# Attention logits on 64 rows of TensorE for each head, in a two-layer decoder trunk on one core

## The chip, the cores and the metric

The kernel runs on one core of a Trainium2 chip. A core has TensorE (PE, the matrix engine; PEld are its weight loads), VectorE (DVE), ScalarE (ACT), GpSimd (POOL) and the queue that issues transfers (SP). The metric is the device time of one launch in microseconds (us); lower is better. Where a number of several runs is given, it is the median.

## The reference

The program is a trunk of two layers on one sequence of 1024 tokens with 1024 channels. Layer 0 is dilated sliding-window attention, layer 1 a state-space layer, each with a gate and with a norm before and behind it. The change is in the logits of layer 0 alone. There are 16 heads of 64 channels and three groups of windows; each group has its own queries, keys and values.

```
DILATED_GROUPS = ((128, 1), (512, 4), (2048, 16))
...
proj = h @ w_in
for g, (window, dilation) in enumerate(DILATED_GROUPS):
    # query t attends to t - j*dilation, j = 0..window/dilation
    logits = einsum('bnqrhe,bnkrhe->bnrhqk', q, k) * HEAD_DIM ** -0.5 + bias
    lse = logsumexp(logits);  p = exp(logits - lse);  o = p @ v
wts = softmax(stack(lses))            # over the three groups
o = sum(wts * outs);  return (o * silu(z)) @ w_out
```

## The kernel before

All matrix products are computed in parts: an operand x is split into a rounded part hi and a rest lo, and a product is hi·hi + hi·lo + lo·hi, three passes of PE (`split`, L79, makes the parts: ACT copies hi, DVE subtracts to get lo).

After a first stage that makes all values (about the first 350 us), `attn_pair` (L652) runs for p = 0 to 7, a pair of heads each, and in it three window groups g. A group projects the queries and then the keys of its two heads: two halves of 512 tokens each, and for a half 24 matmuls of 512 columns in `proj_part` (L110), into a bank of the two-bank pool `psj`. A bank comes free again when `evac_q` (L190) or `evac_k` (L204) has copied it out. The 128 partitions of such a bank are the 64 channels of the first head and the 64 of the second.

`evac_q` and `evac_k` lay the parts out so that one matmul over 128 rows does two of the products. For g = 0 and 1, the tile `qh` holds in its rows the hi part of head 0 above the lo part of head 0, and `ql` the lo part of head 1 above the hi part of head 1; `kh[:, s]` holds the hi keys of head s twice, one copy in each half of the rows, and `kl[:, s]` the lo keys of head s in its own half and zeros in the other. For g = 2 both heads' queries lie one above the other, and the keys of a head have zeros in the other head's rows (`zero_other`, L217, on POOL). `c.kh` and `c.kl` are one buffer each, used by every group in turn.

`attn_unit` (L463) makes the logits of four query tiles of 128 tokens (j = 0 to 3), twice for each group. A tile sees 256 keys, or 128 at a window's edge. For g = 0 and 1 it takes four matmuls (L485), two for each head; for g = 2 three, over both heads at once. They write one bank of the two-bank pool `psl`. DVE then adds the bias and takes the maximum (L488), ACT does the exponential (L499), PE transposes the weights (L510), ACT and DVE split them (`split_weights`), and PE multiplies them with the values (L559, L585).

The order on each engine is made by a scheduler from the program's dependencies and its own estimates; what stands in `with c.tc.high_priority(AHEAD)` is taken earlier than its place in the program. Every engine then works through its own list in order. In the list, projections of a later group fill PE between the logits, transposes and value products of an earlier one. Behind the last pair stands the gate (L800, L801), whose projections also use `psj`.

Of the kernel before, what the change touches and what calls it, by code (L numbers as in the profile page):

```python
# [15 lines left out]
F32 = mybir.dt.float32  # L16
# [24 lines left out]
def f32(ap):  # L41
    return ap.bitcast(F32)
# [146 lines left out]

def evac_q(c, ps, g, t0, q):  # L190


    nc = c.nc
    n = ps.shape[1] // ORD[g]
    at = (S - t0) // ORD[g] - n
    sv = ps.rearrange("p (l r) -> p r l", r=ORD[g])[:, :, ::-1]
    q = [t.rearrange("p (r l) -> p r l", r=ORD[g])[:, :, at:at + n] for t in q]
    a, b = HEADS
# [5 lines left out]
def evac_k(c, ps, g, t0, kh, kl):  # L204


    n = ps.shape[1] // ORD[g]
    at = t0 // ORD[g]
    sv = ps.rearrange("p (l r) -> p r l", r=ORD[g])
# [7 lines left out]
def zero_other(c, t):  # L217

    for s in range(2):
        rows = HEADS[1 - s]  # L220
        c.nc.gpsimd.tensor_copy(t[rows, s, :], c.zt[rows].to_broadcast([64, S]))


def load_first(c, a, k):
# [233 lines left out]
def ms_col(g, n, h, qt):  # L458

    return (n * 16 + h * 8 + 7 - qt, n * 16 + h * 8 + (qt ^ 1), n * 16 + h * 8 + qt)[g]  # L460


def attn_unit(c, g, u, q, k, v, bt, ms, O):  # L463


    nc = c.nc
    qh, ql = q
    kh, kl = k
    lg = c.attn.tile([P, 2, 4, 256], F32, tag="lg", name="lg", bufs=3)
    tiles = []  # L470
    for j in range(4):
        qt = u * 4 + j
        m = (7 - qt, 1 - qt % 2, 0)[g]
        start = (max(m - 1, 0) * P, qt // 2 * 256, qt * P)[g]
        w = 256 if m else 128
        tiles.append(w)
        ps = c.psl.tile([P, 2, 256], F32, tag="psl", name="psl")
        qs = slice(qt * P, qt * P + P)
        ks = slice(start, start + w)
# [6 lines left out]
        for h in range(2):  # L486
            col = ms_col(g, 0, h, qt)
            nc.vector.tensor_tensor_reduce(  # L488
                lg[:, h, j, 0:w], ps[:, h, 0:w], bt[:, h, 256 - w:256], scale=1.0, scalar=-3.0e38,
                op0=ALU.add, op1=ALU.max, accum_out=ms[:, col:col + 1])  # L490
    nm = c.small.tile([P, 2, 4], F32, tag="nm", name="nm")
    at = (4 - 4 * u, 4 * u, 4 * u)[g]
    mx = ms[:, 0:16].rearrange("p (h t) -> p h t", h=2)[:, :, at:at + 4]
    nc.vector.tensor_scalar(nm, mx, -1.0, None, op0=ALU.mult)  # L494
    for h in range(2):
        for j, w in enumerate(tiles):
            col = ms_col(g, 1, h, u * 4 + j)
            b = (3 - j, j ^ 1, j)[g]
            nc.scalar.activation(lg[:, h, j, 0:w], lg[:, h, j, 0:w], AF.Exp, bias=nm[:, h, b:b + 1],  # L499
                                 accum_out=ms[:, col:col + 1])  # L500
    (pv_last if g == 2 else pv_first)(c, g, u, lg, v, O)
    if u == 1:
        put_ms(c, g, ms)
# [148 lines left out]
def attn_pair(c, p, w_in, h):  # L652
    nc = c.nc
    c.pair = p
    O = []
    for g in range(3):
        qh = c.attn.tile([P, S], F32R, tag="qh", name="qh", bufs=2)
        ql = c.attn.tile([P, S], F32R, tag="ql", name="ql", bufs=2)
        w = load_w(c, w_in[g * 8 + p])
        for th in range(2):  # L660
            src = proj_half(c, w, h[th])
            with c.tc.high_priority(AHEAD):
                evac_q(c, src, g, th * H, (qh, ql))
        bt = load_bias(c, p, g)
        if g == 2:
            zero_other(c, c.kh)
        w = load_w(c, w_in[(3 + g) * 8 + p])
        for th in range(2):
            src = proj_half(c, w, h[th])
            with c.tc.high_priority(AHEAD):  # L670
                evac_k(c, src, g, th * H, c.kh, c.kl)
        v = load_v(c, p, g)
        rotations(c, p, g)
        if g == 1:
            run_merge(c)
        ms = c.small.tile([P, 32], F32, tag="ms", name="ms")
        for u in range(2):
            attn_unit(c, g, u, (qh, ql), (c.kh, c.kl), v, bt, ms, O)
# [31 lines left out]
def attention(c, a):  # L710
# [8 lines left out]
    with tc.tile_pool(name="vphase", bufs=1, side="right", reuse_waits="tile") as pool:  # L719
# [21 lines left out]

        v_phase(c, a, rows)

    c.attn = c.es_attn.enter_context(tc.tile_pool(name="attn", bufs=1, side="right", reuse_waits="tile"))
    c.kh = c.attn.tile([P, 2, S], F32R, tag="kh", name="kh")
    c.kl = c.attn.tile([P, 2, S], F32R, tag="kl", name="kl")
    zt = c.cst.tile([P, 1], F32, name="zt")
    nc.vector.memset(zt, 0.0)
    c.zt = zt
    zero_other(c, c.kl)  # L750
    c.w_engine = nc.gpsimd
    for p in range(8):
        attn_pair(c, p, a["w_in"], h)
# [702 lines left out]
def trunk(tc, a):  # L1456
# [4 lines left out]
    with ExitStack() as es:  # L1461
# [8 lines left out]
        c.psl = pool("psl", bufs=2, space=PSUM)  # L1470
        c.pst = pool("pst", bufs=2, space=PSUM)
        c.pso = pool("pso", bufs=2, space=PSUM)
        c.dr = pool("dr", bufs=1, space=DRAM)
        dram = lambda name, shape: c.dr.tile(shape, F32, name=name)
        c.vec_dr = dram("vec_dr", [3, 16, 384])
# [24 lines left out]
        c.es_attn = es.enter_context(ExitStack())  # L1500
        h = attention(c, a)
        c.es_attn.close()
        c.pb = es.enter_context(tc.tile_pool(name="pb", bufs=1, side="right", reuse_waits="tile"))
        g, raw = attn_gate(c, a, h)
        z112 = c.outs.tile([P, D], F32, tag="O", name="z112", bufs=4)[:, 0:8 * 112]
# [111 lines left out]
```

## Time and profile before

| | |
|---|---|
| median of 3 runs | 1727.71 us (1724.31 to 1729.69) |
| profiled execution: time, span | 1722.86 us, 1721.1 us |
| PE busy | 1655.9 us, 96% of the span |
| DVE, ACT, POOL busy | 1064.8, 799.9, 483.5 us |
| attention stage | about 350 to 1156 us |

The span is the time from the first to the last instruction of the profiled execution. In the rows further down a line names the source line, the engine, the operation, the tile written and the tiles read, and after that the shape. For matmuls a pair like 128*128 stands before the shape: the rows and columns of PE that the instruction uses. A matmul's duration contains its way through the array, so that durations of neighbours overlap; the distance from one start to the next tells what it occupies.

### The profile page before, as it was taken

The page shows a single profiled execution, that of the slowest core. Times are in us where ns is not written, and L with a number is a line of the kernel's source. Part 1 is how long each engine was busy: PE and PEld are TensorE (multiplying, and loading weights), DVE is VectorE, ACT ScalarE, POOL GpSimd, SP SyncE. Part 2 cuts the span into 40 slices and gives each one's busy share as a digit, 9 for nine tenths or more (in the row PEclk, how much of TensorE's full clock was granted, in tenths as well). Part 3 has the DMA queues.
Part 4 walks back from the last instruction along what each step waited for, and adds up shares of the span by engine and source line. Part 5 has one row for each costly group of instructions (what it writes and reads, how often), then busy time and mean ns, then how long its engine had stood idle before and what let it go on. Part 6 is the DMA issues. An engine that isn't in the chain of part 4 may idle for free. (4 is left out here: it accounts for less than half of the span.)

```text
span 1721.1 us, 25792 instructions
## 1 busy us (share of the span) xinstructions
PE 1655.9 (96%) x9262; PEld 1415.1 (82%) x9262; DVE 1064.8 (62%) x2582; ACT 799.9 (46%) x1872; POOL 483.5 (28%) x321
## 2 busy tenths in 40 slices
PE   6999999999999999999999999988998999989998
PEld 5889999988888788888888888876886887867886
DVE  7698798735566556566555565557462777764533
ACT  5232222246656656656756756653442232243411
POOL 2000000041242432524342442405210344413121
PEclk9999999999999999999999999999999999999999
DMA  6223454441242323323232423327259766465432
GB/s 236 91 52 102 137 181 154 128 144 53 55 111 80 87 80 91 88 74 105 79 107 73 116 81 98 112 71 200 86 166 232 206 211 219 139 186 167 141 122 86
DMA packets 176900, 212.68 MB, mean 124 GB/s; under 512 B 37361, under 2 KB 133380, under 8 KB 176772
## 3 DMA queue, kind: packets, MB, share of 16 engines
q1 hardware_dynamic: 176772, 211.04, 40.9%
q8 instruction: 73, 1.20, 0.3%
q14 instruction: 55, 0.45, 0.1%
HBM read 154.03 MB, written 56.96 MB: 123 GB/s over the span
## 5 line engine op out<-in xcount | busy, mean ns | idle before, releaser
L110 PE MATMUL psj<-hh,whi 128*128 128x512 f32 x896 | 360.4, 402 | 16.2 <-ACT kh L214 8.5
L110 PE MATMUL psj<-hh,wlo 128*128 128x512 f32 x896 | 359.6, 402 | 0.3 <-POOL wlo L84 0.3
L110 PE MATMUL psj<-hl,whi 128*128 128x512 f32 x896 | 357.9, 399 | 0.0
L110 PEld LDWEIGHTS psj<-hh,whi 128*128 128x128 f32 x896 | 169.8, 189 | 51.6 <-ACT kh L214 10.6
L84 POOL TENSOR_TENSOR wlo<-wraw,whi 128x1024 fp32r<-128x1024 f32 x48 | 115.4, 2405 | 335.7 <-ACT whi L83 329.4
L110 PEld LDWEIGHTS psj<-hh,wlo 128*128 128x128 f32 x896 | 169.6, 189 | 35.8 <-POOL wlo L84 0.7
L110 PEld LDWEIGHTS psj<-hl,whi 128*128 128x128 f32 x896 | 169.8, 190 | 33.5
L499 ACT ACTIVATE lg<-lg,nm 128x128 f32<-128x128 f32 (+1 forms) x384 | 168.1, 440 | 18.9 <-DVE nm L494 18.0
L83 ACT CAST whi<-wraw 128x1024 fp32r<-128x1024 f32 x80 | 83.8, 1047 | 141.9 <-PE psj L110 97.4
L488 DVE CUSTOM_DVE_ANT_0 lg<-psl,T 128x128 f32<-128x128 f32 (+1 forms) x384 | 115.8, 346 | 53.5 <-PE psl L485 52.1
L84 DVE TENSOR_TENSOR ph<-pt,ph 128x512 fp32r<-128x512 f32 (+2 forms) x160 | 97.2, 621 | 37.4 <-ACT ph L83 35.3
L389 PE MATMUL psq<-whi,v 128*128 128x256 f32 x640 | 118.7, 283 | 0.0
L110 PE MATMUL psj<-h1h,whi 128*128 128x512 f32 (+1 forms) x272 | 107.0, 394 | 10.3 <-DVE z L1402 7.9
L84 DVE TENSOR_TENSOR kl<-psj,kh 64x512 fp32r<-64x512 f32 x96 | 66.0, 688 | 70.7 <-ACT kh L83 70.0
L570 DVE TENSOR_TENSOR O<-O,pso 64x512 f32<-64x512 f32 x64 | 44.2, 691 | 103.3 <-ACT O L569 102.6
L110 PE MATMUL psj<-h1l,whi 128*128 128x512 f32 (+1 forms) x272 | 105.4, 388 | 0.2 <-DVE h1l L84 0.2
L110 PE MATMUL psj<-h1h,wlo 128*128 128x512 f32 (+1 forms) x272 | 105.0, 387 | 0.0
L389 PEld LDWEIGHTS psq<-whi,v 128*128 128x128 f32 x640 | 99.5, 189 | 1.0 <-ACT whi L83 0.6
L83 ACT CAST ph<-pt 128x512 fp32r<-128x512 f32 (+2 forms) x160 | 81.6, 533 | 35.9 <-PE pt L510 34.7
L510 PE MATMUL pt<-identr,lg 128*128 128x128 f32 x560 | 93.5, 275 | 0.0
L559 PE MATMUL pso<-ph,vs 128*128 128x256 f32 (+1 forms) x544 | 89.9, 275 | 2.8 <-ACT ph L83 1.5
L559 PEld LDWEIGHTS pso<-ph,vs 128*128 128x128 f32 x544 | 81.6, 189 | 13.1 <-ACT ph L83 2.6
(287 smaller groups left out, 3862.7 us busy)
## 6 DMA issues: line engine op xcount, KB each, us to landing
wraw<-in_w_in_dram SPq DMA_DIRECT2D x56, 512.0 KB
mw<-wt_dr SPq DMA_DIRECT2D x48, 256.0 KB
v<-in_w_v_dram SPq DMA_DIRECT2D x20, 512.0 KB
vp<-v_dr SPq DMA_DIRECT2D x16, 512.0 KB
wraw<-in_ssm_w_in_dram SPq DMA_DIRECT2D x16, 512.0 KB
v_dr<-v SPq DMA_DIRECT2D x30, 256.0 KB
rot_dr<-rt SPq DMA_DIRECT2D x48, 128.0 KB
ca_dr<-ca SPq DMA_DIRECT2D x32, 144.0 KB
```

The lines of the kernel that those rows point to most:

```text
L83: nc.scalar.copy(hi, src)
L84: return (engine or nc.vector).tensor_tensor(lo, src, f32(hi), op=ALU.subtract)
L110: nc.tensor.matmul(ps, a[:, s], b[:, k, :], start=first and k == 0 and n == 0, stop=k == KT - 1 and n == 2, skip_group_check=True)
L389: nc.tensor.matmul(o, r[x][:, k, ts], w[y][:, k, :], skip_group_check=True, start=i in (0, 4, 5) and t % 2 == k == n == 0, stop=k == 3 and ...
L488: nc.vector.tensor_tensor_reduce(lg[:, h, j, 0:w], ps[:, h, 0:w], bt[:, h, 256 - w:256], scale=1.0, scalar=-3.0e38, op0=ALU.add, op1=ALU.m ...
L499: nc.scalar.activation(lg[:, h, j, 0:w], lg[:, h, j, 0:w], AF.Exp, bias=nm[:, h, b:b + 1], accum_out=ms[:, col:col + 1])
L510: c.nc.tensor.transpose(pt[:, n * P:(n + 1) * P], lg[:, h, j, part * P:part * P + P], c.ident)
L559: nc.tensor.matmul(o, l, r, start=n == 0, stop=n == len(jobs) - 1, skip_group_check=True)
L570: nc.vector.tensor_tensor(dst, dst, fr[1], op=ALU.add)
```

## The change

The queries and the keys are split once, as they come: `qh`, `ql`, `kh`, `kl` hold the hi and the lo part of both heads, head 0 in rows 0 to 63 and head 1 in rows 64 to 127. Copies, crosswise halves and zeros are gone. A matmul of the logits reads the 64 rows of one head; the three products of a tile and the two heads make six matmuls, which alternate between the two halves of the rows. The two heads write two different banks of one tile `psl` of two banks, of which there is one buffer (`psa`). For g = 0 and 1 one such tile takes two query tiles, for g = 2 four, and all matmuls into it stand under `high_priority`. `kh` and `kl` become two buffers each, made anew for each group. The pool `psl` of the other stages is closed before the attention and opened again behind it, so that the banks are the same in number.

```
 def evac_q(c, ps, g, t0, q):
...
+    hi, lo = (t.rearrange("p (r l) -> p r l", r=ORD[g])[:, :, at:at + n] for t in q)
+    split(c, hi, lo, ps.rearrange("p (l r) -> p r l", r=ORD[g])[:, :, ::-1], 0.125)
-    for dh, dl, src in (((q[0], q[1], sv),) if g == 2 else ((q[0][a], q[0][b], sv[a]), (q[1][b], q[1][a], sv[b]))):
-        nc.scalar.activation(dh, src, AF.Copy, scale=0.125)
-        nc.vector.scalar_tensor_tensor(dl, src, 0.125, f32(dh), op0=ALU.mult, op1=ALU.subtract)
...
+def evac_k(c, ps, g, t0, k):
...
+    split(c, hi, lo, ps.rearrange("p (l r) -> p r l", r=ORD[g]))
-    for s in range(2):
-        dh, dl = (t[:, s, :].rearrange("p (r l) -> p r l", r=ORD[g])[:, :, at:at + n] for t in (kh, kl))
-        split(c, dh[HEADS[s]], dl[HEADS[s]], sv[HEADS[s]])
-        if g < 2:
-            c.nc.scalar.copy(dh[HEADS[1 - s]], sv[HEADS[s]])
...
 def attn_unit(c, g, u, q, k, v, bt, ms, O):
...
-    for j in range(4):
-        ps = c.psl.tile([P, 2, 256], F32, tag="psl", name="psl")
-        if g == 2:
-            jobs = [(ps[:, :, 0:w], a, b[:, :, ks]) for a, b in ((qh, kh), (qh, kl), (ql, kh))]
-        else:
-            jobs = [(ps[:, h, 0:w], (qh, ql)[h], b[:, h, ks]) for h in range(2) for b in (kh, kl)]
-        for n, (o, a, b) in enumerate(jobs):
-            nc.tensor.matmul(o, a[:, qs], b, start=n == 0, stop=n == len(jobs) - 1, skip_group_check=True)
+    for js in ((0, 1, 2, 3),) if g == 2 else ((0, 1), (2, 3)):
+        psl = c.psa.tile([P, 2, H], F32, tag="psl", name="psl")
...
+        with c.tc.high_priority(AHEAD):
+            for j, o, qs, ks in parts:
+                for n, (x, y) in enumerate(((qh, kl), (ql, kh), (qh, kh))):
+                    for h in range(2):
+                        nc.tensor.matmul(psl[:, h, o], x[HEADS[h], qs], y[HEADS[h], ks],
+                                         start=j == js[0] and n == 0, stop=n == 2, skip_group_check=True)
...
 def attn_pair(c, p, w_in, h):
...
-        if g == 2:
-            zero_other(c, c.kh)
+        kh = c.attn.tile([P, S], F32R, tag="kh", name="kh", bufs=2)
+        kl = c.attn.tile([P, S], F32R, tag="kl", name="kl", bufs=2)
```

How the instructions move, at three places. On PE, in the first pair, g = 0, second unit, the third and fourth query tile (256 and 128 keys). Before:

```order
L110 MATMUL psj_4145<-hh1_111,whi_4110 128x512
L485 MATMUL psl_3956<-kh_3684,qh_3690 128x256
L485 MATMUL psl_3956<-kl_3685,qh_3690 128x256
L485 MATMUL psl_3956<-kh_3684,ql_3691 128x256
L485 MATMUL psl_3956<-kl_3685,ql_3691 128x256
L110 MATMUL psj_4145<-hl1_112,whi_4110 128x512
L485 MATMUL psl_3963<-kh_3684,qh_3690 128x128
L485 MATMUL psl_3963<-kl_3685,qh_3690 128x128
L485 MATMUL psl_3963<-kh_3684,ql_3691 128x128
L485 MATMUL psl_3963<-kl_3685,ql_3691 128x128
L110 MATMUL psj_4145<-hh1_111,wlo_4111 128x512
```

The same two tiles after the change ("x2": one matmul for each head):

```order
L110 MATMUL psj_4386<-hl0_110,whi_4382 128x512
L469 MATMUL psl_3953<-kl_3753,qh_3688 128x256 x2
L469 MATMUL psl_3953<-kh_3752,ql_3689 128x256 x2
L469 MATMUL psl_3953<-kh_3752,qh_3688 128x256 x2
L469 MATMUL psl_3953<-kl_3753,qh_3688 128x128 x2
L469 MATMUL psl_3953<-kh_3752,ql_3689 128x128 x2
L469 MATMUL psl_3953<-kh_3752,qh_3688 128x128 x2
L546 MATMUL pso_3876<-ph_3882,vs_3816 128x256 x3
```

Eight matmuls in two pieces become twelve in one piece. Over the whole program 704 matmuls of logits in 166 pieces become 1152 in 80, 64 of 12 and 16 of 24; each of the 80 stands behind a projection, and behind it stands a value product (48 times), a projection (16) or a transpose (16).

On ACT, the first group's evacuation of the queries' second half and of the keys (`whi` are split weights; the line of dots stands for the same two copies once more). Before:

```order
L83 CAST whi_4044<-wraw_4042 128x1024
L200 ACTIVATE qh_3690<-psj_3727 64x512
L200 ACTIVATE ql_3691<-psj_3727 64x512
L83 CAST kh_3684<-psj_3764 64x512
L214 CAST kh_3684<-psj_3764 64x512
...
L83 CAST whi_4110<-wraw_4108 128x1024
L83 CAST kh_3684<-psj_3795 64x512
L214 CAST kh_3684<-psj_3795 64x512
```

And after:

```order
L83 CAST whi_4044<-wraw_4042 128x1024
L86 ACTIVATE qh_3688<-psj_3723 128x512
L83 CAST kh_3752<-psj_3760 128x512
L83 CAST whi_4108<-wraw_4106 128x1024
L83 CAST kh_3752<-psj_3787 128x512
```

A half of keys takes one copy on ACT in place of four (of two for g = 2), a half of queries one in place of two (one as before for g = 2); DVE's subtractions go from two to one in the same way.

On DVE, at the end of the attention (`cm` are the weights that merge the three groups, which wait for a trip through memory; `gl` are the lo parts of the gated output; `tz` frees a bank of the gate's projection). Before:

```order
L84 TENSOR_TENSOR gl1_11624<-fz_11706,gh1_11623 128x4x64
L623 TENSOR_TENSOR cm2_1519<-cm0_1517 64x32
L84 TENSOR_TENSOR gl0_11622<-fz_11714,gh0_11621 128x512
L624 TENSOR_TENSOR cm2_1519<-cm2_1519,cm0_1517 64x32
L84 TENSOR_TENSOR gl1_11624<-fz_11718,gh1_11623 128x512
L625 TENSOR_TENSOR cm1_1518<-cm0_1517,cm2_1519 64x96
L801 SCALAR_TENSOR_TENSOR tz_11798<-tz_11798,psj_11773 128x512
```

And after:

```order
L610 TENSOR_TENSOR cm2_1519<-cm0_1517 64x32
L611 TENSOR_TENSOR cm2_1519<-cm2_1519,cm0_1517 64x32
L612 TENSOR_TENSOR cm1_1518<-cm0_1517,cm2_1519 64x96
L614 TENSOR_TENSOR cm0_1517<-cm0_1517,cm1_1518 64x3x32
L615 TENSOR_TENSOR cm2_1519<-cm0_1517 64x32
L616 TENSOR_TENSOR cm2_1519<-cm2_1519,cm0_1517 64x32
L577 COPY O2_11645<-pso_11726 64x256
L617 RECIPROCAL cm2_1519<-cm2_1519 64x32
L84 TENSOR_TENSOR gl0_11768<-fz_11808,gh0_11767 128x4x64
```

The merge weights move ahead of the last copy of the attention's output. On PE the transposed row sums (`ptm`) that they wait for stand five matmuls before the last value product in the program before; after the change some twenty projection matmuls lie between, and eleven projection matmuls that need no new bank stand behind it.

## Rows read from the trace of the kernel before

**Rows 1.** The page's part 1: busy time of the engines, share of the span.

```profile
PE 1655.9 (96%) x9262; PEld 1415.1 (82%) x9262; DVE 1064.8 (62%) x2582; ACT 799.9 (46%) x1872; POOL 483.5 (28%) x321
```

**Rows 2.** Busy time in the attention stage: span, PE, PEld, DVE, ACT, POOL, clock, DMA.

```profile
350.00:1156.00 806.00, 794.60 (x4424) 679.20 (x4423) 454.99 (x1333) 511.01 (x1371) 287.57 (x160) 1.00 0.31 88
```

**Rows 3.** PE's longest waits: us in total, times, longest us.

```profile
PE psj L110 <- ACT kh L214: 8.5, 4, 2.6
...
PE psj L110 <- DVE tz L801: 7.7, 1, 7.7
```

**Rows 4.** The matmuls of line L485, by operands: duration, first and last start, forms.

```profile
L485 PE MATMUL psl<-kh,qh x192: 218/280/368, 372.9 to 1141.6; 128*128 128x256 f32 x152, 128*128 128x128 f32 x40
...
L485 PE MATMUL psl<-kl,qh x192: 273/280/368, 373.0 to 1141.7; 128*128 128x256 f32 x152, 128*128 128x128 f32 x40
...
L485 PE MATMUL psl<-kh,ql x192: 221/281/367, 373.4 to 1141.8; 128*128 128x256 f32 x152, 128*128 128x128 f32 x40
...
L485 PE MATMUL psl<-kl,ql x128: 273/281/367, 373.5 to 1111.4; 128*128 128x256 f32 x88, 128*128 128x128 f32 x40
```

**Rows 5.** PE in order of time, 714.9 to 716.4: start us, duration us, instruction.

```profile
715.15 0.28 PE L485 MATMUL psl<-kh,qh 128*128 128x256 f32 x1
715.27 0.28 PE L485 MATMUL psl<-kl,qh 128*128 128x256 f32 x1
...
715.63 0.22 PE L485 MATMUL psl<-kh,qh 128*128 128x128 f32 x1
...
716.03 0.45 PE L110 MATMUL psj<-hh,wlo 128*128 128x512 f32 x1
716.31 0.39 PE L110 MATMUL psj<-hh,whi 128*128 128x512 f32 x1
```

**Rows 6.** PE in order of time, 155.3 to 156.95.

```profile
155.51 0.28 PE L389 MATMUL psq<-whi,v 128*128 128x256 f32 x1
155.72 0.81 PE L175 MATMUL psb<-oneh,relx 33*16 33x384 f32 x2
156.46 0.39 PE L389 MATMUL psq<-whi,hh 128*128 128x256 f32 x1
156.69 0.27 PE L389 MATMUL psq<-wlo,hh 128*128 128x256 f32 x1
156.80 0.28 PE L389 MATMUL psq<-whi,hl 128*128 128x256 f32 x1
```

**Rows 7.** PE in order of time, 208.4 to 209.5, and one row from 211.0 on.

```profile
208.53 0.28 PE L389 MATMUL psq<-whi,hl 128*128 128x256 f32 x1
208.74 0.41 PE L1214 MATMUL pk<-ca,O 128*32 128x128 f32 x2
209.08 0.33 PE L1226 MATMUL ptb<-identr,zr 128*128 128x128 f32 x1
209.16 0.37 PE L389 MATMUL psq<-whi,hh 128*128 128x256 f32 x1
209.36 0.28 PE L389 MATMUL psq<-wlo,hh 128*128 128x256 f32 x1
...
211.21 1.61 PE L1214 MATMUL pk<-ca,O 128*32 128x128 f32 x13
```

**Rows 8.** Groups by line and shape: count, busy us, mean ns, idle before and its cause.

```profile
L83 ACT CAST kh<-psj 64x512 fp32r<-64x512 f32 x96 | 55.8, 582 | 32.6 <-PE psl L485 17.0 <-DVE kl L84 12.2 <-PE psj L110 2.4
...
L214 ACT CAST kh<-psj 64x512 fp32r<-64x512 f32 x64 | 37.1, 580 | 34.6 <-DVE kl L84 34.1
...
L488 DVE CUSTOM_DVE_ANT_0 lg<-psl,T 128x256 f32<-128x256 f32 x176 | 66.6, 419 | 42.0 <-PE psl L485 41.0
```

**Rows 9.** DVE in order of time, at the end of the attention stage.

```profile
1157.34 2.63 DVE L84 TENSOR_TENSOR gl<-fz,gh 128x256 fp32r<-128x256 f32 x6
1161.66 0.18 DVE L623 TENSOR_TENSOR cm<-cm 64x32 f32<-64x32 f32 x1 [1.69 <-DMA cm<-ms_dr]
...
1163.35 0.69 DVE L801 SCALAR_TENSOR_TENSOR tz<-tz,psj 128x512 f32<-128x512 f32 x1
```

More of the change, by code (lines that the diff above doesn't have):

```diff
@@ L190, in evac_q @@
 def evac_q(c, ps, g, t0, q):
[L193 removed]
     n = ps.shape[1] // ORD[g]
     at = (S - t0) // ORD[g] - n
[L196 to L204 removed]
+    hi, lo = (t.rearrange("p (r l) -> p r l", r=ORD[g])[:, :, at:at + n] for t in q)
+    split(c, hi, lo, ps.rearrange("p (l r) -> p r l", r=ORD[g])[:, :, ::-1], 0.125)
+def evac_k(c, ps, g, t0, k):
     n = ps.shape[1] // ORD[g]
     at = t0 // ORD[g]
[L209 to L221 removed]
+    hi, lo = (t.rearrange("p (r l) -> p r l", r=ORD[g])[:, :, at:at + n] for t in k)
+    split(c, hi, lo, ps.rearrange("p (l r) -> p r l", r=ORD[g]))
 def load_first(c, a, k):
@@ L470, in attn_unit @@
     tiles = []
-    for j in range(4):
[L472 to L476, printed above, removed]
-        ps = c.psl.tile([P, 2, 256], F32, tag="psl", name="psl")
-        qs = slice(qt * P, qt * P + P)
-        ks = slice(start, start + w)
-        if g == 2:
-            jobs = [(ps[:, :, 0:w], a, b[:, :, ks]) for a, b in ((qh, kh), (qh, kl), (ql, kh))]
-        else:
-            jobs = [(ps[:, h, 0:w], (qh, ql)[h], b[:, h, ks]) for h in range(2) for b in (kh, kl)]
-        for n, (o, a, b) in enumerate(jobs):
-            nc.tensor.matmul(o, a[:, qs], b, start=n == 0, stop=n == len(jobs) - 1, skip_group_check=True)
[L486 to L490, printed above, removed]
+    for js in ((0, 1, 2, 3),) if g == 2 else ((0, 1), (2, 3)):
+        psl = c.psa.tile([P, 2, H], F32, tag="psl", name="psl")
+        parts, at = [], 0
+        for j in js:
+            qt = u * 4 + j
+            m = (7 - qt, 1 - qt % 2, 0)[g]
+            start = (max(m - 1, 0) * P, qt // 2 * 256, qt * P)[g]
+            w = 256 if m else 128
+            tiles.append(w)
+            parts.append((j, slice(at, at + w), slice(qt * P, qt * P + P), slice(start, start + w)))
+            at += w
+        with c.tc.high_priority(AHEAD):
[4 more added lines that the diff above has]
+                                         start=j == js[0] and n == 0, stop=n == 2, skip_group_check=True)
+        for j, o, _, _ in parts:
+            w = tiles[j]
+            for h in range(2):
+                col = ms_col(g, 0, h, u * 4 + j)
+                nc.vector.tensor_tensor_reduce(
+                    lg[:, h, j, 0:w], psl[:, h, o], bt[:, h, 256 - w:256], scale=1.0, scalar=-3.0e38,
+                    op0=ALU.add, op1=ALU.max, accum_out=ms[:, col:col + 1])
     nm = c.small.tile([P, 2, 4], F32, tag="nm", name="nm")
@@ L670, in attn_pair @@
             with c.tc.high_priority(AHEAD):
-                evac_k(c, src, g, th * H, c.kh, c.kl)
+                evac_k(c, src, g, th * H, (kh, kl))
         v = load_v(c, p, g)
@@ L677, in attn_pair @@
         for u in range(2):
-            attn_unit(c, g, u, (qh, ql), (c.kh, c.kl), v, bt, ms, O)
+            attn_unit(c, g, u, (qh, ql), (kh, kl), v, bt, ms, O)
             if p and g == u == 0:
@@ L742, in attention @@
         v_phase(c, a, rows)
+    c.es_ps.close()
+    c.psa = c.ps("psa", 1)
     c.attn = c.es_attn.enter_context(tc.tile_pool(name="attn", bufs=1, side="right", reuse_waits="tile"))
[L745 to L750, printed above, removed]
     c.w_engine = nc.gpsimd
@@ L1469, in trunk @@
         c.psj = pool("psj", bufs=2, space=PSUM)
-        c.psl = pool("psl", bufs=2, space=PSUM)
         c.pst = pool("pst", bufs=2, space=PSUM)
         c.pso = pool("pso", bufs=2, space=PSUM)
+        c.es_ps = es.enter_context(ExitStack())
+        c.ps = lambda name, bufs: c.es_ps.enter_context(tc.tile_pool(name=name, bufs=bufs, space=PSUM, reuse_waits="tile"))
+        c.psl = c.ps("psl", 2)
         c.dr = pool("dr", bufs=1, space=DRAM)
@@ L1502, in trunk @@
         c.es_attn.close()
+        c.es_ps.close()
+        c.psl = c.ps("psl2", 2)
         c.pb = es.enter_context(tc.tile_pool(name="pb", bufs=1, side="right", reuse_waits="tile"))
```

## The prediction, made before the changed kernel ran

> **What bounds the kernel now.** I read the page's busy times first: PE is busy for 96% of the span, the next engine for 62% [rows 1]. The logits are made in the attention stage, and there PE is busy for 794.6 of 806 us, ACT for 511 and DVE for 455 [rows 2]. So an engine other than PE can only matter where PE waits for it. PE's list of waits names two that the change touches [rows 3]: 8.5 us in four waits, the longest 2.6 us (so three of about that), where a projection waits for a bank that ACT has not emptied because it still copies keys (L214), and a single 7.7 us where a projection of the gate waits for DVE (L801). Everything else is PE's own work. The question is then how long PE needs for the logits, before and after.
>
> **Logits before.** The forms of L485 give 152 + 152 + 152 + 88 = 544 matmuls of 256 columns and 4 × 40 = 160 of 128 [rows 4]. A wide one takes 0.12 us from start to start (715.15 to 715.27, and four in the 0.48 us to 715.63). Four narrow ones take 0.40 us, and the projection behind them takes 0.28 us to its successor, where 512 columns at the pace of the wide ones would take 0.24: 0.44 for four, 0.11 each [rows 5]. So half the columns save almost nothing: the narrow matmul waits for its weights, whose load takes about 0.11 us. Sum: 544 × 0.12 + 160 × 0.11 = 65.3 + 17.6 = 82.9 us.
>
> **Logits after.** For a pair of heads, group 0 has 7 tiles of 256 keys and one of 128, group 1 four and four, group 2 eight of 128: 11 wide and 13 narrow. With three products and eight pairs that is 264 wide and 312 narrow couples, a couple being the two heads' matmuls on the two halves of the rows. The trace of before has no such couple. Its price is bounded from below by one matmul (both halves load and stream at once) and from above by two (one after the other). At the lower end the logits take 264 × 0.12 + 312 × 0.11 = 31.7 + 34.3 = 66.0 us, 16.9 less than now; at the upper end 132.0 us, 49.1 more. I take the lower end: the halves read different rows, write different banks and have nothing to wait for in each other, and in one of the few visits to a smaller piece of the array (L1214, 128*32) thirteen matmuls run in 1.61 us; less the last one's 0.27 that is 0.112 each, so loads hide under matmuls there too [rows 7].
>
> The Trainium skill says under "TensorEngine Tiling (Array Packing)", Key Properties, that different tiles of the array can execute weight loads and matmuls in parallel. No run here shows it yet; by it the lower end holds.
>
> **Going into that mode and out.** The change also adds what the old logits never needed: PE goes 80 times from whole-array matmuls to half-row ones and back. The trace has two kinds of such visits, both in the stage before. At L1214 the matmul ahead starts at 208.53 and the first narrow-array one at 208.74: 0.21 instead of 0.12. Then two matmuls, a transpose, a matmul, up to 209.36: 0.83 us in all, against 0.12 + 2 × 0.11 + 0.11 + 0.12 = 0.57 without a visit. A visit costs 0.26 us there, with a load of only 32 columns on the way in [rows 7]. At L175 (33*16) the way in is 0.21 instead of 0.12 again (155.51 to 155.72), and on the way out the first whole-array matmul takes 0.23 us to the next, which then takes 0.11 [rows 6]: its full-width load of 0.11 us lay open, since it could not start under the matmul ahead. The new runs load full widths on both ways. So: way in 0.09 + 0.11, way out 0.09 + 0.11, together 0.40 us; where a transpose stands behind (16 times) the way out shows only 0.05 more at its successor (209.08 to 209.36 is 0.28 instead of 0.23), 0.34 together. Sum: 64 × 0.40 + 16 × 0.34 = 31.0 us. From below I bound it by the cheaper visit, 80 × 0.26 = 20.8 us. I take 31.0, since the loads are as wide as those of [rows 6].
>
> **Waits that go.** The copies of keys: ACT needs 0.58 us for each of the 96 and 64 half-height copies [rows 8], four to a half of keys, and they alternate with DVE's subtractions. One copy and one subtraction remain, and with two buffers they no longer wait for the logits of the group before (17.0 us of ACT's idle time there is put down to L485 [rows 8]). I take the three long waits as gone, 8.2 us; what is late next is the projection's own weights, which POOL splits well ahead. Ends: 0 and 8.5. The work that ACT, DVE and POOL lose otherwise lies under PE and counts nothing. **The end of the stage:** DVE stands behind the merge weights (1.69 us of waiting for memory at 1161.66) before it frees a bank at 1163.35 [rows 9]. In the new order the row sums leave PE some twenty projections (20 × 0.24 = 4.8 us) earlier, but eight pieces of `gl` now stand between, where six take 2.63 us [rows 9], and eleven projection matmuls (2.6 us) fill PE meanwhile. I count about 6.6 us until the bank is free, less 2.6: 4 us of waiting in place of 7.7. I take 3.5 us as gained; ends 0 and 4.
>
> **A wait that is added.** There is one two-bank tile, so a run cannot start before DVE has read the last one: four reads of at most 0.42 us each and a short one behind each [rows 8], some 2 us, with a piece or two of other work ahead. Between two runs PE has at least fourteen projections, seven transposes and ten value products: 14 × 0.24 + 7 × 0.11 + 10 × 0.12 = 5.3 us. Taken at nothing; if that cover failed by half a microsecond at 64 runs, it would be 32 us.
>
> **Sum.** -16.9 + 31.0 - 8.2 - 3.5 = +2.4 us. The profiled execution's 1722.86 becomes 1725.3; it lies 4.85 under the median of the runs shown, so the median 1727.71 becomes 1730. By the ends of the terms, with the halves in parallel: -16.9 + 20.8 - 8.5 - 4 = -8.6 (1719) to -16.9 + 31.0 + 0 + 0 + 5 for small new waits = +19 (1747).
>
> **Rivals.** *The halves don't run at once*, because their loads go one after the other or the matmuls do: +49.1 + 31.0 - 11.7 = +68 us, 1796; with the cheap visits 1786. For it: in the trace, loads follow each other at 0.11 us and narrow matmuls are held to that. Against it: those loads go to the same rows. It decides for slower from the point where a couple costs 0.125 us: the sum is then 2.8 us higher (2.8 / 576 couples = 0.005), 0.3% over before.
>
> *Loads hide only under the other half.* A load would have to wait for its own half's matmul, so a couple costs load and matmul in turn, 0.11 + 0.12 wide and 0.11 + 0.06 narrow: 264 × 0.23 + 312 × 0.17 = 113.7 us, so +30.8 + 31.0 - 11.7 = +50, 1778. Against it stands L1214, where loads hide under matmuls on the same piece of the array [rows 7]. The Trainium skill states under "TensorE: Matmul & The Clock Gate", The mechanism, that in packed matmuls a load overlaps one in flight only if the row group differs; by that rule this case holds, and the rows of before differ from it.
>
> *DVE late with its reads*: 1762 by the price above. Against it: DVE is busy for 455 of 806 us and loses its second subtractions.
>
> *Cheap visits*: if the drain between the modes is shorter for row halves than for the two kinds seen, say 0.15 us a visit, the sum is -16.9 + 12 - 11.7 = -17, 1711. Against it: both kinds show at least 0.26.
>
> That the change doesn't do what it says, runs broken up by other work, is excluded by the order: all 80 are whole.
>
> **How the numbers follow.** A measurement can tell about 0.3%, 5.2 us, from no change. Parallel halves with visits as priced: 0.53, of which 0.05 faster, 0.33 within, 0.15 slower. One after the other: 0.25. Loads only under the other half: 0.05. DVE late: 0.05. Cheap visits: 0.12, of which 0.10 faster and 0.02 within. So faster 0.15, within 0.35, slower 0.50. The likeliest single case is the sum, 1730, with its own range 1719 to 1747. The range for 8 in 10 has to reach to the serial case: 1713 to 1796 leaves out half of the cheap visits (0.06) and the upper part of the serial case (about 0.1).
>
> **What would show it.** In the trace after: starts of the two heads' matmuls a few hundredths of a us apart and the next couple 0.12 later confirm parallel halves; equal distances of 0.11 to 0.12 are the serial case. The distance from the last projection to the first logit (0.33 instead of 0.24) and the first distances behind a run (0.2 more in all) show the visits. The list of PE's waits should have lost the copies of keys and half the wait at the gate, and should name no wait for L475's reads. Wrong the prediction would be above all by the couple's price, then by the visit's.

## The result and the profile after

| | before | after |
|---|---|---|
| median of 4 runs | 1727.34 us (1724.31 to 1729.69) | 1703.09 us (1702.50 to 1707.17) |
| profiled execution: time, span | 1722.86, 1721.1 us | 1703.36, 1701.6 us |
| first logit, last logit, last matmul start at | 372.9, 1141.8, 1712.6 us | 371.0, 1123.8, 1693.1 us |

The ratio is 0.9866, with a 95% interval of 0.9844 to 0.9888: the changed kernel is 1.3% faster. The first and last logits of after are these rows' (those of before stand in [rows 4]):

```profile
L469 PE MATMUL psl<-kl,qh x384: 216/277/384, 371.0 to 1123.6; 64*128 64x128 f32 x104, 64*128 64x256 f32 x88
...
L469 PE MATMUL psl<-kh,qh x384: 268/273/285, 371.4 to 1123.8; 64*128 64x128 f32 x104, 64*128 64x256 f32 x88
```

The prediction, 1730 us in a range of 1713 to 1796, was wrong in size and in sign.

Busy time of the engines, the page's part 1, as in [rows 1]:

```profile
PE 1651.8 (97%) x9710; PEld 1399.3 (82%) x9710; DVE 1012.8 (60%) x2501; ACT 711.9 (42%) x1728; POOL 461.6 (27%) x303
```

The attention stage as in [rows 2] (length, busy time of PE, PEld, DVE, ACT and POOL, clock, DMA share):

```profile
350.00:1156.00 806.00, 802.61 (x4878) 667.76 (x4877) 408.19 (x1275) 429.33 (x1242) 271.09 (x145) 1.00 0.32 91
```

PE is busy for 8 us more of the same 806 us, ACT for 82 us less. PE's longest waits, as in [rows 3], from the top of the list (us in total, times, longest):

```profile
PE pst L125 <- DVE v L138: 12.2, 1, 12.2
PE psj L110 <- DVE z L1385: 8.8, 4, 3.9
PE psb L110 <- ACT g0b L83: 5.2, 2, 4.9
PE pv L1327 <- DMA U<-u_dr: 3.5, 1, 3.5
PE psj L110 <- DVE tz L784: 3.4, 1, 3.4
```

The copies of keys, 8.5 us before, are gone from the list. The bank of the gate (L801 before, L784 now) costs 3.4 us in place of 7.7. Nothing waits for L475, DVE's reads of the two-bank tile.

The first run of logits, PE in order of time (start, duration; x2 is one matmul of each head). The number 64*128 is the piece of the array that is used:

```profile
370.46 0.39 PE L110 MATMUL psj<-hl,whi 128*128 128x512 f32 x1
370.69 0.40 PE L110 MATMUL psj<-hh,wlo 128*128 128x512 f32 x1
371.01 0.39 PE L469 MATMUL psl<-kl,qh 64*128 64x256 f32 x2
371.24 0.28 PE L469 MATMUL psl<-kh,ql 64*128 64x256 f32 x2
371.35 0.28 PE L469 MATMUL psl<-kh,qh 64*128 64x256 f32 x2
371.47 0.28 PE L469 MATMUL psl<-kl,qh 64*128 64x256 f32 x2
371.58 0.28 PE L469 MATMUL psl<-kh,ql 64*128 64x256 f32 x2
371.70 0.28 PE L469 MATMUL psl<-kh,qh 64*128 64x256 f32 x2
371.91 0.50 PE L110 MATMUL psj<-hh,whi 128*128 128x512 f32 x1
372.25 0.39 PE L110 MATMUL psj<-hl,whi 128*128 128x512 f32 x1
```

Its weight loads:

```profile
371.01 0.18 PEld L469 LDWEIGHTS psl<-kl,qh 64*128 64x128 f32 x2 [0.36 <-issue]
371.12 0.19 PEld L469 LDWEIGHTS psl<-kh,ql 64*128 64x128 f32 x2
```

Here almost all of the prediction's reading of PE can be seen. The six couples start 0.11 to 0.12 us apart, as single matmuls did [rows 5]; the two heads' starts within a couple differ mostly by 2 to 5 ns in the trace, by 10 ns at most. The way in is 0.32 (370.69 to 371.01) where projections follow each other at 0.23; the first couple takes 0.23 in place of 0.12, since its load lies open (0.36 us without a load). The way out is 0.21 (371.70 to 371.91) in place of 0.12, and the first projection behind it 0.34 (371.91 to 372.25) in place of 0.23. That is 0.09 + 0.11 + 0.09 + 0.11 = 0.40 us, the price that the prediction took from [rows 6]. A run takes from its first couple to the next instruction 0.833 us (40 runs), 0.907 (24 runs, all wide, as above) or 1.485 (16 runs of g = 2), nearly the same each time. 40 × 0.833 + 24 × 0.907 + 16 × 1.485 = 78.9. The way in adds 0.095 to each of 80 runs. The first distance behind a run is 0.11 longer than usual 50 times; it is only 0.055 longer the 30 times that a transpose or a value product of 128 columns stands there. 78.9 + 7.6 + 5.5 + 1.7 makes 93.7 us, 11 more than the 82.9 of before. The prediction had 97.0.

**So PE's own work grew, as predicted, and the kernel still became faster.** The gain has to be in waits. In the profiled pair it divides into 1.9 us ahead of the first logit, where nothing was changed, 16.2 between the first logit and the last (769.0 to 752.8), and 1.4 behind. Of the 16.2, 7.4 are only moved: 2259 projections stand between first and last logit before, 2227 after, and 32 × 0.23 us are done behind. What remains, 8.8 us less in spite of 11 us more of work, says that some 20 us of waits went, not 8.2.

The trace of before has them, more than half of them outside of the row that the prediction used. That row is the waits for copies of keys, three of which look like this:

```profile
596.56 0.50 PE L110 MATMUL psj<-hh,whi 128*128 128x512 f32 x1 [2.57 <-ACT kh L214]
596.90 0.39 PE L110 MATMUL psj<-hl,whi 128*128 128x512 f32 x1
597.13 0.40 PE L110 MATMUL psj<-hh,wlo 128*128 128x512 f32 x1
```

PE in order of time behind 396 us, in the kernel before:

```profile
396.09 0.40 PE L110 MATMUL psj<-hh,wlo 128*128 128x512 f32 x1
397.94 0.39 PE L559 MATMUL pso<-ph,vs 128*128 128x256 f32 x1 [1.45 <-ACT ph L83]
398.91 0.63 PE L559 MATMUL pso<-ph,vs 128*128 128x256 f32 x3 [0.58 <-DVE ph L84]
...
400.27 0.60 PE L110 MATMUL psj<-hh,wlo 128*128 128x512 f32 x1
400.67 0.63 PE L110 MATMUL psj<-hh,whi 128*128 128x512 f32 x1
401.10 0.63 PE L110 MATMUL psj<-hl,whi 128*128 128x512 f32 x1
```

The same stretch by windows (the clock is the number ahead of the DMA share):

```profile
396.00:400.00 4.00, 1.97 (x12) 1.32 (x11) 1.74 (x3) 3.93 (x13) 0.00 (x0) 1.00 0.01 2
400.00:404.00 4.00, 4.00 (x12) 3.10 (x12) 2.23 (x4) 3.06 (x6) 2.99 (x2) 0.57 0.00 0
```

and after:

```profile
400.00:404.00 4.00, 4.00 (x26) 3.62 (x27) 3.05 (x11) 2.03 (x4) 0.00 (x0) 1.00 0.09 25
```

In before, value products wait for split weights, and behind that gap the granted clock is 0.57, near the lower of the two levels, 1.2 of 2.4 GHz: projections stand 0.43 apart in place of 0.23, with PE counted as fully busy. Eight such steps cost 1.6 us that are in no list of waits. A gap alone does not bring this: behind the 2.57 us ahead of 596.56 the projections stand 0.23 apart again from the second on. Between first and last logit I took each start-to-start distance on PE beyond the median of its kind (the kind is the line and shape of a matmul and of the one behind it): before has eight excesses of over 0.5 us, together 12.8, and 22.0 us of smaller ones over 0.05. A kernel with the same shapes of matmuls and no waits (b_both, below) has none of the first and 15.4 of the second. 12.8 + 22.0 - 15.4 = 19 us. Of these, 9.1 stand at the four waits for copies of keys, 3.7 at split weights, and 6.6 are small. The small ones depend on where one starts to count: with all of them in, the difference is 19 to 21.

### The profile page after: what moved, and what is told of

The parts are those of the page before. It is cut to its first block, busy times and chain, and to the rows that moved or that the text cites. A ratio compares the mean times of both kernels' runs of the same rounds, so it can differ in the third digit from the quotient of the medians.

```text
span 1701.6 us, 26274 instructions
## 1 busy us (share of the span) xinstructions
PE 1651.8 (97%) x9710; PEld 1399.3 (82%) x9710; DVE 1012.8 (60%) x2501; ACT 711.9 (42%) x1728; POOL 461.6 (27%) x303
## 5 line engine op out<-in xcount | busy, mean ns | idle before, releaser
L475 DVE CUSTOM_DVE_ANT_0 lg<-psl,T 128x128 f32<-128x128 f32 (+1 forms) x384 | 110.6, 347 | 89.8 <-PE psl L469 89.8
L84 DVE TENSOR_TENSOR kl<-psj,kh 128x512 fp32r<-128x512 f32 x48 | 33.2, 692 | 117.2 <-ACT kh L83 116.7
L371 PE MATMUL psq<-wlo,v 128*128 128x256 f32 x320 | 90.0, 282 | 2.2 <-DVE wlo L84 2.2
L1201 POOL TENSOR_TENSOR Ks<-Ks,O 32x64 f32<-32x64 f32 x8 | 4.6, 574 | 296.5 <-ACT Ks L1199 280.8
L497 PE MATMUL pt<-identr,lg 128*128 128x128 f32 x560 | 82.2, 277 | 0.0
```

What stands on the lines that cost most here:

```text
L371: nc.tensor.matmul(o, r[x][:, k, ts], w[y][:, k, :], skip_group_check=True, start=i in (0, 4, 5) and t % 2 == k == n == 0, stop=k == 3 and ...
L475: nc.vector.tensor_tensor_reduce(lg[:, h, j, 0:w], psl[:, h, o], bt[:, h, 256 - w:256], scale=1.0, scalar=-3.0e38, op0=ALU.add, op1=ALU.ma ...
L497: c.nc.tensor.transpose(pt[:, n * P:(n + 1) * P], lg[:, h, j, part * P:part * P + P], c.ident)
L1201: nc.gpsimd.tensor_tensor(Ks[:, :, 0:16], Ks[:, :, 0:16], self.dd, op=ALU.add)
```

## The experiments

Theory A: the half-row runs cost PE what the prediction said; the gain comes from waits that go, because keys leave their bank after one copy and because logits come early. Theory B: the half-row runs themselves are cheap or even gain. Further theories came up on the way and stand with their runs. Medians below are set against the before of the same batch (1726.72 to 1727.66 us); "after" is 1703.09.

### Whole-array logits in the same places

The edit to after in a_whole; g = 2 takes three matmuls over 128 columns of both heads.

```
             for j, o, qs, ks in parts:
-                for n, (x, y) in enumerate(((qh, kl), (ql, kh), (qh, kh))):
-                    for h in range(2):
-                        nc.tensor.matmul(psl[:, h, o], x[HEADS[h], qs], y[HEADS[h], ks],
...
+                    jobs = [(psl[:, h, o], x, y[:, ks]) for h, x in enumerate((qh, ql)) for y in (kl, kh)]
+                for n, (t, x, y) in enumerate(jobs):
...
+                    nc.tensor.matmul(t, x[:, qs], y, start=first, stop=n == 2 if g == 2 else n % 2 == 1, skip_group_check=True)
```

> The changed kernel with whole-array matmuls in place of the couples: four a tile for groups 0 and 1 and three of 256 columns for group 2, as many as before the change, in the same 80 runs, with the queries and keys split once and two key buffers. Each logit then sums both heads, so the output is another one; the work of the other engines stays. Theory A (the couples and the 80 visits to half-row mode together cost PE about 12 us more than the old matmuls did, and the gain lies in waits of PE that went): about 1703 - 12 = 1691 us, between 1687 and 1694. Rival B (visits cost little, the couples are the gain): 1703 + 17 = 1720 us.

Measured: 1698.55 us (1696.03 to 1699.67), ratio 0.9831 (0.9799 to 0.9864), faster than after, but outside of both expectations. From first logit to last it takes 741.4 us where after takes 752.8, with six projections more in the stretch (6 × 0.23 = 1.4): couples and visits cost 12.8 us over whole-array matmuls, near the 11 counted above and the prediction's 14.1. The total shows only 4.5 of it, as the part behind the last logit takes 576.3 us in place of 569.3 (more on that under the single key buffer). Theory B is out: the half-row form of the logits is a loss by itself.

### The price of a visit, alone

A whole-array matmul of zeros is added to each run of after, in its middle (a_zero_mid, shown) or at its end (a_zero_end, where the condition is `i == len(parts) - 1`).

```
+                if i == len(parts) // 2 - 1:
+                    _, o, _, ks = parts[0]
+                    nc.tensor.matmul(psl[:, 0, o], c.zw, kh[:, ks], start=False, stop=True, skip_group_check=True)
```

> The changed kernel with one whole-array matmul of zeros added at the end of each of the 80 runs of logits (it adds zero to the first tile). It pays the way out of half-row mode in place of what stood there, so it costs only its own 0.11 to 0.12 us: 80 x 0.12 = 9.6 us, 1713 (1708 to 1717). This kernel is the control of the next one. If the visits cost nothing, the same.

> The same whole-array matmul of zeros, in the middle of each run: every run becomes two visits to half-row mode. Theory A (a visit costs 0.09 + 0.11 us on each way, as in rows 6 of the kernel before): 80 x 0.40 = 32 us over the control, about 1744 (1736 to 1750). Rival (a visit between full-width loads costs 0.15 us): 12 us over the control, 1725.

Measured: 1718.22 us (1716.26 to 1719.33) and 1750.12 us (1744.94 to 1753.32). Their difference is 31.9 us, 0.40 for each of 80 visits, as expected, though each lies just over the upper end of its own range. Between first and last logit the profiled pair differs by 30.0 us (792.9 against 762.9), with five projections more (1.2), so that a visit is nearer to 0.36 to 0.38; the rest of the difference lies outside of that stretch. The control itself cost 15 in place of 9.6; between first and last logit it is 10.1 (762.9 against 752.8), and 3.1 lie behind. A run of a_zero_mid, PE in order of time:

```profile
372.39 0.28 PE L469 MATMUL psl<-kh,qh 64*128 64x256 f32 x2
372.60 0.38 PE L473 MATMUL psl<-kh,zw 128*128 128x256 f32 x1
372.91 0.39 PE L469 MATMUL psl<-kl,qh 64*128 64x256 f32 x2
373.13 0.28 PE L469 MATMUL psl<-kh,ql 64*128 64x256 f32 x2
```

One whole-array matmul of 0.12 us between couples: 0.21 to it, 0.31 from it, 0.22 for the couple behind, against 0.12 each inside of a run: 0.74 - 3 × 0.12 = 0.38.

### Runs broken up

The edit to after in a_plain:

```
-        with c.tc.high_priority(AHEAD):
-            for j, o, qs, ks in parts:
+        for j, o, qs, ks in parts:
```

> The changed kernel without high priority around the logits: the scheduler breaks the 80 runs into 221 pieces, 53 of them single matmuls. Theory A (a visit costs about 0.39 us): 141 more visits are 55 us, and a single matmul is half a couple that runs alone, up to 0.1 us each, 3 us: about 1760 us, less what the other order hides. Rival B (visits cost little): 1703 to 1715 us.

Measured: 1763.04 us (1753.94 to 1771.17), ratio 1.0208 (1.0161 to 1.0254). Without high priority the scheduler breaks the 80 runs into 221 pieces: 141 visits more at 0.40 make 56 us, and 1703 + 56 = 1759. Visits are nearly the whole loss, and the 53 single matmuls can be the rest. PE shows no idle time between 371 and 1112 us here either, though the logits no longer come early. So in this kernel, with short copies, two key buffers, the tile of two banks and some 59 us more work on PE between first and last logit (811.9 against 752.8), late logits bring no waits back; which of these differences from b_short (below) keeps it free of them is not shown.

### Heads one after the other

The edit to after in a_serial:

```
-            for j, o, qs, ks in parts:
-                for n, (x, y) in enumerate(((qh, kl), (ql, kh), (qh, kh))):
-                    for h in range(2):
+            for h in range(2):
+                for j, o, qs, ks in parts:
+                    for n, (x, y) in enumerate(((qh, kl), (ql, kh), (qh, kh))):
```

> The changed kernel with the two heads one after the other in each run instead of alternating: first all matmuls of head 0, then all of head 1. Theory A (a couple runs in parallel only because the two halves alternate in the one list of PE): the couples fall apart, 264 x 0.12 + 312 x 0.11 = 66 us more, 1769 (1755 to 1778). Rival (PE runs ahead in one half while the other works): 1703 to 1715.

Measured: 1749.26 us (1746.93 to 1750.59), ratio 1.0132 (1.0115 to 1.0150): 46 us over after, between the two. A run, PE in order of time:

```profile
372.32 0.38 PE L469 MATMUL psl<-kl,qh 64*128 64x256 f32 x1
...
372.54 0.28 PE L469 MATMUL psl<-kh,ql 64*128 64x256 f32 x1
...
372.66 0.28 PE L469 MATMUL psl<-kh,qh 64*128 64x256 f32 x1
372.67 0.18 PEld L469 LDWEIGHTS psl<-kl,qh 64*128 64x128 f32 x2
372.67 0.38 PE L469 MATMUL psl<-kl,qh 64*128 64x256 f32 x1
```

Head 1's first matmul stands seventh in the list and starts at 372.67, when head 0's third starts at 372.66, ahead of head 0's fourth to sixth: within PE's list the two halves are not strictly in order, other than the part ahead of the prediction says of every engine. In a run of g = 2 it stands 13th and starts with head 0's ninth. So PE here reaches four places past a matmul that is just starting, into the other half, and in neither kind of run further. Runs take 1.184, 1.249 and 2.435 us in place of 0.833, 0.907 and 1.485: 40 × 0.351 + 24 × 0.342 + 16 × 0.95 = 37 of the 46 us; the other 9 are not explained. Each half takes its own matmuls at 0.12 us, loads hidden under matmuls on the same rows (between 372.54 and 372.66 nothing else runs; in the first run of g = 2, head 0 alone goes at 0.11 from its second matmul to its ninth). Alternating the heads in the list is what lets them overlap fully.

### One key buffer

The edit to after in a_keys1:

```
-        kh = c.attn.tile([P, S], F32R, tag="kh", name="kh", bufs=2)
-        kl = c.attn.tile([P, S], F32R, tag="kl", name="kl", bufs=2)
+        kh = c.attn.tile([P, S], F32R, tag="kh", name="kh", bufs=1)
+        kl = c.attn.tile([P, S], F32R, tag="kl", name="kl", bufs=1)
```

> The changed kernel with one buffer each for the keys' hi and lo parts in place of two. Theory A: PE's waits for a bank that holds keys come back in part, 5 to 15 us: 1708 to 1718 us. Rival B (the second buffer hides nothing that counts, since the evacuation has become short): within 2 us of 1703.

Measured: 1709.73 us (1706.38 to 1710.70), ratio 0.9897 (0.9869 to 0.9925). The total fell where A expected it, but not for A's reason. In the stage nothing changed: PE has no idle time between 371 and 1112 us, and first to last logit is 753.7 against 752.8. The 7 us are behind the last logit, 576.6 in place of 569.3, about half of it (3.5) around one place in the gate's output, up to 1187 us. PE's wait there in this kernel:

```profile
PE pso L838 <- ACT gh L83: 3.9, 1, 3.9
```

against 1.9 in after, with a granted clock of 0.84 against 0.87 between 1150 and 1190 us. ACT there waits for POOL (`fz`), which this edit doesn't touch. The other half comes in steps of up to 1.5 us further on, with a granted clock of 0.93 against 0.97 between 1300 and 1350 us and 0.97 against 0.99 between 1400 and 1500. Two similar lengths of the part behind the last logit come up in other kernels: 569 to 572 us in before, after, b_short, a_plain, a_serial and a_zero_end; 576 to 578 in a_keys1, a_whole, b_both, b_ahead, b_runs_dup and a_zero_mid; b_runs (582.9) and c_long (597.0) are longer. Which one a kernel gets is not explained by anything tried here. Each kernel has one trace, and one of after's own four runs took 1707.17 us, so it isn't even shown that the length belongs to the kernel. The second key buffer hides nothing in the stage; whether it is what shifts the gate stays open.

### Where the waits come from: short copies, early logits, both

Three variants of the kernel before, all with whole-array logits and one key buffer. b_short has the first of the two edits below (and the like in `evac_q`), b_ahead the second, b_both has both.

```
 def evac_k(c, ps, g, t0, kh, kl):
...
+    hi, lo = (t[:, 0, :].rearrange("p (r l) -> p r l", r=ORD[g])[:, :, at:at + n] for t in (kh, kl))
+    split(c, hi, lo, ps.rearrange("p (l r) -> p r l", r=ORD[g]))
-    for s in range(2):
-        dh, dl = (t[:, s, :].rearrange("p (r l) -> p r l", r=ORD[g])[:, :, at:at + n] for t in (kh, kl))
-        split(c, dh[HEADS[s]], dl[HEADS[s]], sv[HEADS[s]])
-        if g < 2:
-            c.nc.scalar.copy(dh[HEADS[1 - s]], sv[HEADS[s]])
```

```
+        with c.tc.high_priority(AHEAD):
             for n, (o, a, b) in enumerate(jobs):
                 nc.tensor.matmul(o, a[:, qs], b, start=n == 0, stop=n == len(jobs) - 1, skip_group_check=True)
```

> The kernel before with the short evacuation alone: queries and keys are split once, full height, into the first half of the key tiles, and the logits (still whole-array matmuls, still one bank for a query tile, still without high priority, still one buffer for the keys) read that half, so that each logit sums over both heads; the output is another one for that reason. Theory A: the waits of PE in the attention stage of the kernel before came from the long chain of copies that holds a projection bank, so they go here too, and the time is 1708 to 1718. Theory B: they came from the order of the work (logits late in the list), so PE still waits in pieces of 2 us or more, and the time is 1722 to 1728.

> The kernel before the change, with only its logits' matmuls taken earlier by high priority, as the changed kernel takes them. Theory A: the wait for the single key buffer and the long evacuation stay; 1720 to 1728 us. Rival C (the new order of the program, fewer and larger pieces, is the gain): 1705 to 1712 us.

> The kernel before with two edits together that gave nearly nothing singly: the short evacuation (queries and keys split once, so that each logit sums over both heads and the output is another one) and high priority for the logits. Logits stay whole-array, in one bank for a query tile, with one key buffer. Theory A (PE's waits had two causes, of which either is enough to keep them: logits late in the list, and copies that hold the projection bank): both are gone, 1700 to 1712. Theory B (the uninterrupted runs into two banks are what matters): 1716 to 1726.

| | before | b_short | b_ahead | b_both |
|---|---|---|---|---|
| median, us | 1726.72 to 1727.66 | 1724.70 | 1723.56 | 1708.55 |
| ratio to before (95%) | 1 | 0.9987 (0.9976 to 0.9999) | 0.9979 (0.9961 to 0.9996) | 0.9889 (0.9865 to 0.9913) |
| PE idle between 371 and 1112, us | 11.3 | 7.9 | 11.0 | 0.0 |
| excess distances over 0.5 us, first to last logit | 12.8 in 8 | 11.3 in 12 | 12.6 in 8 | none |

Each edit alone gives 2 to 4 us, both together 18. What stays in b_short, from PE's waits:

```profile
PE pso L551 <- ACT ph L83: 6.1, 8, 1.6
...
PE pso L551 <- DVE ph L84: 3.1, 9, 0.6
```

in b_ahead:

```profile
PE pso L560 <- ACT ph L83: 5.5, 3, 1.9
...
PE psj L110 <- ACT kh L214: 3.7, 2, 3.2
```

and in b_both the window from 371 to 1112 us:

```profile
371.00:1112.00 741.00, 741.00 (x4189) 640.73 (x4188) 371.09 (x1217) 401.79 (x1172) 272.74 (x149) 1.00 0.31 89
```

With short copies alone, projections no longer wait for the copies of keys, but value products then wait for their split weights. One such place in b_short, first PE, then ACT:

```profile
619.02 0.27 PE L477 MATMUL psl<-kl,ql 128*128 128x128 f32 x1
...
625.03 0.38 PE L551 MATMUL pso<-ph,vs 128*128 128x256 f32 x1 [1.59 <-ACT ph L83]
```

```profile
620.40 0.51 ACT L491 ACTIVATE lg<-lg,nm 128x256 f32<-128x256 f32 x1 [3.39 <-DVE nm L486]
...
624.40 0.85 ACT L83 CAST ph<-pt 128x512 fp32r<-128x512 f32 x2
```

ACT sits idle for 3.39 us until the next unit's logits, which PE ends at 619.02, have their maximum; it then does that unit's exponentials, and only behind them in its list the copy of weights that PE waits for. With early logits alone, copies of keys still stand between the split weights on ACT (in b_ahead, L214 at 399.26 between the copies of `ph` at 398.15 and 399.86), and both kinds of waits stay. Theory A of b_both holds: either cause alone leaves PE waiting, and both edits together leave it no wait. My expectation that short copies alone would do it fell. That late logits bring waits with short copies is shown for this form of the kernel; a_plain is a form without them.

### The early runs with the long copies

b_runs is the kernel before with after's tile `psl` of two banks and its loop over `js` under high priority, and these matmuls for g = 0 and 1:

```
+                    jobs = [(psl[:, h, o], x, y[:, h, ks]) for h, x in enumerate((qh, ql)) for y in (kl, kh)]
```

b_runs_dup is b_runs with one line of `evac_k` changed:

```
-            c.nc.scalar.copy(dh[HEADS[1 - s]], sv[HEADS[s]])
+            c.nc.scalar.copy(dh[HEADS[1 - s]], f32(dh[HEADS[s]]))
```

> The kernel before with the logits of the changed kernel's order: two query tiles (four for g = 2) into one tile of two banks, under high priority, but whole-array matmuls with before's doubled keys, before's long evacuation and one key buffer. Theory A (the long evacuation alone keeps PE waiting): waits for the copies of keys (L214) and for split weights stay, 1714 to 1726. Theory B (the order alone removes them): 1697 to 1706.

> The kernel b_runs with one edit: the second copy of the keys is taken from the first copy and no longer from the projection bank, so that the bank is held for two copies of ACT instead of four. ACT has as much work as before. If the time that the bank is held makes the waits: 5 to 12 us under b_runs. If it is ACT's work as such (copies of weights and outputs come late behind it): within 3 us of b_runs.

Measured: 1752.49 us (1750.96 to 1754.17), ratio 1.0147 (1.0123 to 1.0172), and 1740.61 (1738.84 to 1742.99), ratio 1.0079 (1.0054 to 1.0104). Both expectations for b_runs missed: after's order of logits on the old copies is not neutral but 26 us slower than before. PE's waits in b_runs:

```profile
PE pso L568 <- DVE ph L84: 13.2, 11, 2.4
...
PE psj L110 <- ACT kh L214: 5.2, 8, 1.4
```

It is idle for 20.9 of the 741 us, at a mean clock of 0.97. Against a_whole, the same runs with short copies and two key buffers, that is 54 us. How much of it is the buffers' is not shown: a_keys1 tried them with short copies alone. Taking only the second copy away from the bank gives 11.9 back, by ACT's unchanged amount of work, as expected if the bank's time counts. But the idle time is no shorter (21.8 of the 741 us): the waits for L214 are gone from the list, waits for the queries' lo part (DVE `ql`, 11.8 us in 7) stand in their place, and the gain shows in a mean clock of 0.99 in place of 0.97. So the number came as forecast, the reason for it is not shown.

### Longer runs

c_long is after with `pst` and `pso` of one bank each in the attention, and this edit:

```
-    for js in ((0, 1, 2, 3),) if g == 2 else ((0, 1), (2, 3)):
-        psl = c.psa.tile([P, 2, H], F32, tag="psl", name="psl")
+    for js in ((0, 1, 2, 3),):
+        psl = c.psa.tile([P, 2, 2 * H], F32, tag="psl", name="psl")
```

> The changed kernel with all four query tiles of a unit in one run, into a tile of four banks; the banks come from the transposes and the value products, which keep one each instead of two. 48 runs instead of 80, so 32 visits fewer. If the single banks cost nothing (between two uses stand projections): 32 x 0.40 = 12.8 us under the changed kernel, 1690 (1686 to 1695). If each use of a single bank waits for the copy out of it, half a us at some 100 places: 50 us more, 1715 to 1745.

Measured: 1979.42 us (1974.88 to 1981.03), ratio 1.1455 (1.1420 to 1.1491), far beyond both. PE's waits, and a late part of the stage:

```profile
PE pso L546 <- ACT ph L83: 36.1, 31, 3.1
PE psj L110 <- DVE ql L87: 31.3, 19, 3.0
PE pso L546 <- DVE O L557: 19.2, 8, 3.7
```

```profile
1150.00:1380.00 230.00, 197.06 (x1030) 159.82 (x1031) 91.81 (x293) 98.70 (x293) 52.34 (x27) 0.81 0.24 70
```

With single banks the value products wait for their weights and for the copy out of their bank. Between first and last logit PE sits idle for 124 us, where after has none, and the stretch takes 1004.1 us in place of 752.8; much of the rest is in steps at a lower clock (0.81 in this window). Not all of it is the single banks': 15.3 us of PE's waits are for L475, the reads of the tile of four banks, which the edit also brings. Fewer visits would be worth 12.8 us; the edit as a whole loses some twenty times that.

## Why the prediction was wrong, step by step

- **Logits as couples** (66.0 us, -16.9): right. Starts mostly 2 to 5 ns apart, couples at 0.11 to 0.12. The serial rival (0.25) and the rival of loads that hide only under the other half (0.05) are out; a_serial shows loads hidden under matmuls on the same rows. The Trainium skill's sentence in "TensorEngine Tiling (Array Packing)", Key Properties, that tiles load and multiply in parallel, is borne out by these 2 to 5 ns. The rule of the Trainium skill in "TensorE: Matmul & The Clock Gate", The mechanism, that in packed matmuls a load overlaps one in flight only if the row group differs, is not: one half alone goes at 0.11 in a_serial, where load and matmul in turn would make 0.17.
- **Visits** (31.0 us): right. 80 added visits cost 31.9 us in the medians, 30.0 between first and last logit. The shorter way out comes behind 30 runs, not 16. Couples and visits together were 97.0 predicted, 93.7 counted. Cheap visits (0.15 us) are out.
- **Waits that go** (-8.2, with ends 0 and -8.5): the step that failed; about -19. The 8.2 doesn't follow from the rows either: the three long waits are 2.57, 2.57 and 2.56 us, together 7.7. But the size of the row is not the fault. The prediction said of all but its two rows "Everything else is PE's own work", and took as its bound one row of the list of waits, the copies of keys [rows 3]. That left out the waits of value products for split weights, the small waits, and the stretch at half clock behind a gap, which counts as busy. It also said that the work that ACT, DVE and POOL lose "lies under PE and counts nothing". It did not: PE also waited for split weights, and it stops doing so when the copies are short and the logits early (b_both; short copies alone give 2 us, early logits alone 4, both 18). And it costed the earlier place of the logits at nothing.
- **The end of the stage** (-3.5): right; 7.7 became 3.4.
- **The added wait for the two-bank tile** (nothing): right; L475 is in no list.
- **The base**: the prediction added 4.85 us because before's profiled run lay under its median. After's profiled run lies at its median, so this shift fell away.

The sum of misses: 10.8 for the waits, 3 for the logits, 0.8 for the end, 5 for the base, 6 for differences ahead of the first logit (1.9) and behind the stage (some 4), which no run explains. That is 25.6 of the 27 us between 1730 and 1703.

## What to carry to other kernels

A list of waits by releaser is no upper bound for what shorter work on another engine can give: ask which waits would move into the freed place, count every excess distance on the bound engine, and look for stretches at a lower clock behind gaps. Two edits that each do nearly nothing can make up a gain together, when either cause alone keeps the bound engine waiting. And half-row matmuls pay only if a run saves more than the 0.40 us of going there and back; here they lost 11 us of PE's time, and the short evacuation that they allow, with the logits early, paid for it.

## What the runs showed of the hardware that was not expected

- PE starts matmuls of the other half up to four places ahead in its list while the first half works through its own (a_serial: 372.66 and 372.67).
- A gap can cost more than its length: in before, 1.45 + 0.58 us of waiting was followed by eight projections 0.43 us apart, at a granted clock of 0.57 between 400 and 404 us. It need not: behind the gap of 2.57 us ahead of 596.56 they were 0.23 apart from the second on.
